# Where the sums of MLP weights are made: by transfers ahead of time, or on load, in a hybrid block on one core

## The chip, the core and the metric

The kernel runs on one core of a Trainium2 chip. The metric is the device time in microseconds (us) of one execution. It took 1217.34 us before the change, the median of three runs (1215.89 to 1218.22).

The engines go by the names of the profile: PE is TensorE (its weight loads are PEld), DVE VectorE, ACT ScalarE, POOL GpSimd, and SP the queue from which most transfers are issued. L633 is line 633 of the kernel.

## The reference

One block over a sequence of 1024 tokens with 1024 features, all in 32-bit floating point:

```python
h = rms_norm(x, norm1_g)
x = x + hybrid_mixer(h, ...)            # 8 heads of stick-breaking attention beside an RG-LRU
h = rms_norm(x, norm2_g)
x = x + sq_relu_mlp(h, w_up, w_down)

def hybrid_mixer(h, ...):
    proj = h @ w_in
    q, k, v, xl, gl = jnp.split(proj, ...)
    attn = stick_breaking_attention(rms_norm(q, ...), rms_norm(k, ...), v)
    lru = rg_lru(causal_depthwise_conv(xl, ...), ...) * jax.nn.gelu(gl)
    return jnp.concatenate([attn, lru], axis=-1) @ w_out

def sq_relu_mlp(h, w_up, w_down):
    return jnp.square(jax.nn.relu(h @ w_up)) @ w_down     # 1024 -> 4096 -> 1024
```

## The kernel before

Every product is made in three matmuls: each operand is split in a high part, rounded to TensorE's fast 32-bit type by ACT (L544), and a low part, the rest, by DVE or POOL (L60). A name ending in h or l (`sh_u`, `sl_u`) is such a part. A station (`s...`) is the operand that TensorE loads, a moving operand (`m...`) the one that streams.

The program has four stretches. To 155 us it normalizes x, projects and runs the LRU. From 155 to 462 us attention runs in head pairs, with the rest of the input projection and the gates of the LRU between its steps. From 462 to 566 us comes the output projection, and then the MLP to 1210 us.

The MLP is cut in two groups of 2048 hidden features, and each runs `up_group` and then `down_group`. The product of 2 x 2 blocks is made with seven block products in place of eight, so some products need sums of blocks of the weights. In w_up the blocks are called w(i, j, k): half i of the group's features, tile j of that half, half k of the inputs. `up_group` has four passes over j = 0 to 7:

- p1 (L657 on): stations `a` from w(0, j, 0) and w(0, j, 1), two quarter-products (12 matmuls each) per j.
- p6 and p7: stations `s`. `rs` takes w(1, j, 1) by a load and a ready sum of two blocks by another (L697); POOL adds the two (L698). p6 streams `t2`, p7 `t3`; the low part of half of `t3` is made on POOL.
- p4: stations `t`, a plain load for two j.
- p5 and b22: stations `u`. `ru` and `rv` take four loads, two of them ready sums (L735, L736), and POOL adds all in one instruction of 128x1024 (L737).

The eight sums U of a j are squared on ACT or POOL (L660, L662, L664). `down_group` runs seven products of 96 matmuls (pa, pb, pc); p6, p7 and p4 read ready sums of w_down, and POOL adds `rp` and `qp` (L767).

The ready sums lie in DRAM: `sum_u` and `sum_d`, 2 x 2 MB each for each group. `weight_sum(n)` makes them on POOL's own transfer queue, for each group 4 transfers of 2 MB for w_up and 4 for w_down: the first two copy a block of weights, the other two add a block to what was copied (`accum_op`). Eight of the sixteen, those for group 0, are the steps Y00 to Y07 of the attention part's table ORDER (L34). The other eight, for group 1, are issued in group 0: two in p6 (L699), two in p4 (L715), four in the down products p5 and p6 (L768). Each is issued behind the last POOL instruction that was marked.

`raw` tiles hold what is loaded: a pool of six buffers of 128x1024; split stations rotate through three pairs, moving operands through five. A scheduler orders each engine's instructions by a simulated timeline; in each queue they then run in that order.

The gates (G steps, `gate`, L478) multiply a projection by the row scales 1/rms. The scales lie in DRAM (`rs_d`); `rsb` holds them broadcast over the partitions, but only while the LRU runs, so each of the eight gate steps loads its half of them again into `gx` (L483) before DVE's multiply (L487).

Of the kernel before, what the change touches and what calls it, by code (L numbers as in the profile page):

```python
# [19 lines left out]
P = 128  # L20
S = 1024
# [12 lines left out]
ORDER = (  # L34
# [3 lines left out]
).split()  # L38
# [5 lines left out]
def kernel(ctx, tc, x, norm1_g, w_in, conv_w, conv_b, w_rg, b_rg, w_ig, b_ig,  # L44
# [85 lines left out]

    sums = {("u", g): dram.tile([2, 8, P, 512], F32, name=f"sum_u{g}") for g in range(2)}
    sums.update({("d", g): dram.tile([2, 8 * P, 512], F32, name=f"sum_d{g}") for g in range(2)})

    def weight_sum(n):
        m, g = (("u", 0), ("d", 0), ("u", 1), ("d", 1))[n // 4]
        i, k, dst = ((1, 0, 0), (0, 1, 1), (0, 0, 0), (1, 1, 1))[n % 4] if m == "u" else ((1, 1, 0), (0, 0, 1), (0, 1, 0), (1, 0, 1))[n % 4]

        def rows(w):  # L140
            return w.rearrange("j p c -> (j p) c") if len(w.shape) == 3 else w


        f = 16 * g + 8 * i
        src = rows(w_up[k, f:f + 8] if m == "u" else w_down[k, f * P:(f + 8) * P])
        with tc.issue_after(marked[0]):
            nc.gpsimd.dma_start(rows(sums[m, g][dst]), src, max_dma_last_dim=2048, **({"accum_op": ALU.add} if n % 4 > 1 else {}))

# [3 lines left out]
    hTl = hp.tile([P, KC, S], F32R, name="hTl")  # L152
    qkvE = pool(left1, "qkvE")
    wp = pool(left1, "wp", bufs=8)
    mp = pool(left1, "misc")
# [196 lines left out]
    lp = pool(lstack, "lru", bufs=2, side="right")  # L352
    rsb = lp.tile([P, S], F32, name="rsb", bufs=1)
    for ch in range(2):
# [124 lines left out]
    def gate(c, ch):  # L479
        s0 = 512 * ch  # L480
        y = mp.tile([P, 512], F32, tag="raw", name=f"gx{c}{ch}", bufs=2)
        hs = mp.tile([P, 512], F32, tag=("ks", "kl")[c % 2], name=f"hl{c}{ch}")
        nc.sync.dma_start(y, rs_row[:, s0:s0 + 512].broadcast_to([P, 512]))  # L483
        nc.sync.dma_start(hs, lru_d[c * P:(c + 1) * P, s0:s0 + 512])
        pd = proj_cols(gw[c // 2 * 2], c % 2, ch, f"pgl{c}{ch}")
        t = mp.tile([P, 512], F32, tag=("sq", "qs")[c % 2], name=f"ge{c}{ch}")
        nc.vector.tensor_tensor(y, pd, y, op=ALU.mult)  # L487
        nc.scalar.activation(t, y, AF.Square, scale=math.sqrt(0.044715))
        nc.vector.scalar_tensor_tensor(t, t, 1.0, y, op0=ALU.add, op1=ALU.mult)
        nc.scalar.activation(t, t, AF.Sigmoid, scale=c2)  # L490
        nc.gpsimd.tensor_tensor(hs, hs, y, op=ALU.mult)
        nc.gpsimd.tensor_tensor(hs, hs, t, op=ALU.mult)
        nc.sync.dma_start(mix_d[AW + c * P:AW + (c + 1) * P, s0:s0 + 512], hs)
# [13 lines left out]
    for op, *digits in ORDER:  # L507
# [5 lines left out]
        elif op == "A":  # L513
            attention(*arg, qkvs[arg[0]])
        elif op == "Y":
            weight_sum(10 * arg[0] + arg[1])
        elif op == "W":
            gate_w(*arg)
        else:
            gate(*arg)  # L520
# [123 lines left out]
    def up_group(g):  # L644
        SU = sums["u", g]

# [23 lines left out]
        for j in range(9):  # L670
# [7 lines left out]
            if held is not None:  # L678
                ps, st = held
                mm4(ps, st, 1, b21, False)  # L680
                relu2(j - 1, 0, ps)
            held = cur

# [10 lines left out]
        for j in range(8):  # L694
            r = raw(f"rs{g}{j}")
            nc.sync.dma_start(r[:, 0], w_up[1, 16 * g + 8 + j])
            nc.sync.dma_start(r[:, 1], SU[0, j])  # L697
            mark(nc.gpsimd.tensor_tensor(r[:, 0], r[:, 0], r[:, 1], **add))  # L698
            if g == 0 and j % 4 == 0:  # L699
                weight_sum(8 + j // 4)  # L700
            st = split(nc.vector, pair(stp, f"s{g}{j}"), r)
# [12 lines left out]
        for j in range(8):  # L714
            if g == 0 and j % 4 == 2:  # L715
                weight_sum(10 + j // 4)
            if j % 2 == 0:
# [11 lines left out]
        for j in range(9):  # L729
            cur = None  # L730
            if j < 8:
                r, q = raw(f"ru{g}{j}"), raw(f"rv{g}{j}")
                nc.sync.dma_start(r[:, 0], w_up[0, 16 * g + 8 + j])
                nc.sync.dma_start(q[:, 0], w_up[1, 16 * g + 8 + j])
                nc.sync.dma_start(r[:, 1], SU[1, j])  # L735
                nc.sync.dma_start(q[:, 1], SU[0, j])  # L736
                mark(nc.gpsimd.tensor_tensor(r, r, q, **add))  # L737
                st = split(nc.vector, pair(stp, f"u{g}{j}"), r)
# [14 lines left out]
    def down_group(g):  # L753
        SD = sums["d", g]

# [3 lines left out]
        def product(name, pss, src, unit, start):  # L759

            for k in range(0, 8, 2):
                r = raw(f"r{name}{g}{k}")
                nc.sync.dma_start(r, src[0](k))
                if len(src) > 1:
                    q = raw(f"q{name}{g}{k}")
                    nc.sync.dma_start(q, src[1](k))
                    mark(nc.gpsimd.tensor_tensor(r, r, q, **add))  # L767
                    if g == 0 and name != "p4" and k % 4 == 0:  # L768
                        weight_sum(12 + (2 if name == "p6" else 0) + k // 4)
                mv = split(nc.vector, pair(mvp, f"{name}{g}{k}"), r)  # L770
# [104 lines left out]
```

## Time and profile before

The profiled execution took 1218.14 us. Its span, from its first instruction to its last, is 1216.4 us; 1.7 us lie around it.

| | us |
|---|---|
| median of three runs | 1217.34 |
| profiled execution | 1218.14 |
| its span | 1216.4 |
| front to 155 us | 155.0, TensorE busy 138.25 |
| attention part | 307.0, TensorE busy 292.84 |
| output projection | 104.3, TensorE busy 95.78 |
| MLP group 0 | 332.87, TensorE busy 315.85 |
| MLP group 1 | 311.23, TensorE busy 305.84 |
| POOL busy | 586.5 of the span |
| granted TensorE clock | 0.969 of full speed |

Busy time adds up an engine's instructions; a row with a bracket, such as [8.83 <-issue], gives the idle time in front of an instruction and what ended it, "issue" where the profile shows nothing that the engine waited for. "DMA to landing" is the time from a transfer's issue to its last byte. The transfers of `weight_sum` land a median of 12.7 us (w_up) and 13.3 us (w_down) after their issue.

### The profile page before, as it was taken

What the parts mean: (1) busy time and instruction counts of PE and PEld (TensorE: products, weight loads), DVE (VectorE), ACT (ScalarE), POOL (GpSimd) and SP (SyncE); (2) the same over time, 40 slices, a digit from 0 to 9 for tenths busy, and PEclk for the clock granted to TensorE, in tenths of its full rate; (3) what the DMA queues carried; (4) which work ended last, traced back from release to release, by engine and by line L of the source; (5) the groups of instructions that cost most, each with busy time, mean ns of one, the idle gap of its engine ahead of it and who ended that gap; (6) DMA issues with size and microseconds to landing.
All of it is one profiled execution on the core that took longest, in us unless ns stands there. A gap on an engine that the chain in (4) does not pass through costs nothing.

```text
span 1216.4 us, 15273 instructions
## 1 busy us (share of the span) xinstructions
PE 1150.6 (95%) x5410; PEld 948.0 (78%) x5410; DVE 897.3 (74%) x1182; ACT 568.5 (47%) x991; POOL 586.5 (48%) x472
## 2 busy tenths in 40 slices
PE   7998899999999988998999989889999999999998
PEld 7976777789987766886888767678887887878887
DVE  6889997999898788226387769685843876699663
ACT  7554475665665564144433554233334335733331
POOL 1356764574355566102645746533317368483240
PEclk9999999799999978998999989989999999999999
DMA  8110026824505275200453788944412345442531
GB/s 262 48 49 35 18 96 130 227 66 145 122 5 112 89 256 181 101 1 35 141 188 130 201 241 287 224 142 139 141 35 87 122 144 191 158 148 73 193 132 69
DMA packets 91659, 157.05 MB, mean 129 GB/s; under 512 B 8848, under 2 KB 27328, under 8 KB 91584
## 3 DMA queue, kind: packets, MB, share of 16 engines
q1 hardware_dynamic: 79040, 122.54, 30.5%
q0 software_dynamic: 12544, 33.56, 11.8%
q8 instruction: 42, 0.69, 0.2%
q14 instruction: 33, 0.27, 0.1%
HBM read 145.58 MB, written 44.04 MB: 156 GB/s over the span
## 4 chain that ended last, share of the span: by engine, by line
PE 69%; DVE 13%; issue 8%; DMA 3%; POOL 3%; ACT 3%; SPq 0%; DVEq 0%; ACTq 0%; POOLq 0%
PE p L633 22%; PE pa L633 11%; PE pb L633 5%; PE pc L633 4%; PE pd L71 3%; PE pd L72 3%; PE pd L73 3%; PE po L71 3%; PE po L72 2%; PE po L73 2%; PE av L461 2%; PE z L432 2%; PE pw L452 2%; DVE g L441 2%; DVE sl_u L60 2%
## 5 line engine op out<-in xcount | busy, mean ns | idle before, releaser
L442 POOL TENSOR_TENSOR w<-w,g 128x128 f32<-128x128 f32 (+3 forms) x96 | 99.7, 1044 | 107.7 <-DVE g L441 52.7
L60 DVE TENSOR_TENSOR ml_p<-rp,mh_p 128x1024 fp32r<-128x1024 f32 x56 | 110.3, 1971 | 28.1 <-ACT mh_p L544 28.1
L441 DVE TENSOR_TENSOR_SCAN g<-g 128x128 f32<-128x128 f32 (+3 forms) x96 | 112.6, 1185 | 8.0 <-ACT g L436 5.4
L544 ACT CAST sh_p<-U 128x1024 fp32r<-128x1024 f32 x48 | 50.5, 1051 | 131.0 <-PE pa L633 59.2
L633 PE MATMUL pa<-mh_p,sl_p 128*128 128x512 f32 x256 | 100.7, 393 | 7.1 <-DVE sl_p L60 6.8
L767 POOL TENSOR_TENSOR rp<-rp,qp 128x1024 f32<-128x1024 f32 x24 | 69.0, 2876 | 70.3 <-DMA qp<-in_w_down_dram 39.8
L633 PE MATMUL pa<-ml_p,sh_p 128*128 128x512 f32 x256 | 100.3, 392 | 0.0
L633 PE MATMUL pa<-mh_p,sh_p 128*128 128x512 f32 x256 | 100.1, 391 | 0.0
L71 PE MATMUL pd<-wh_p,hTl 128*128 128x384 f32 x256 | 90.9, 356 | 7.3 <-DVE vv L206 5.0
L72 PE MATMUL pd<-wl_p,hTh 128*128 128x384 f32 x256 | 89.8, 351 | 0.1
L73 PE MATMUL pd<-wh_p,hTh 128*128 128x384 f32 x256 | 88.3, 345 | 0.0
L60 DVE TENSOR_TENSOR sl_p<-U,sh_p 128x1024 fp32r<-128x1024 f32 x38 | 63.4, 1668 | 30.7 <-ACT sh_p L544 30.7
L737 POOL TENSOR_TENSOR ru<-ru,rv 128x1024 f32<-128x1024 f32 x16 | 43.8, 2769 | 58.9 <-DMA rv<-sum_u 58.8
L544 ACT CAST mh_p<-rp 128x1024 fp32r<-128x1024 f32 x56 | 58.7, 1048 | 21.3 <-POOL rp L767 14.6
L633 PEld LDWEIGHTS pa<-mh_p,sl_p 128*128 128x128 f32 x256 | 48.5, 189 | 18.2 <-DVE sl_p L60 7.5
L662 POOL TENSOR_TENSOR U<-U 128x512 f32<-128x512 f32 x32 | 47.0, 1501 | 32.0 <-ACT U L660 32.0
L456 ACT CAST wth<-pw 128x512 fp32r<-128x512 f32 (+1 forms) x80 | 42.4, 545 | 38.0 <-PE pw L452 24.8
L436 ACT ACTIVATE g<-z 128x384 f32<-128x384 f32 (+3 forms) x96 | 47.8, 497 | 22.9 <-PE z L434 10.4
L71 PEld LDWEIGHTS pd<-wh_p,hTl 128*128 128x128 f32 x256 | 49.4, 193 | 11.0 <-DVE vv L206 6.7
L660 ACT ACTIVATE U<-U 128x512 f32<-128x512 f32 x48 | 30.0, 628 | 58.6 <-DVE U L721 31.1
L60 DVE TENSOR_TENSOR wtl<-pw,wth 128x512 fp32r<-128x512 f32 (+1 forms) x80 | 49.5, 629 | 9.5 <-ACT wth L456 8.9
L633 PEld LDWEIGHTS pa<-mh_p,sh_p 128*128 128x128 f32 x256 | 48.5, 189 | 10.2
(325 smaller groups left out, 3566.7 us busy)
## 6 DMA issues: line engine op xcount, KB each, us to landing
sum_u<-in_w_up_dram POOLq DMA_DIRECT2D x8, 2048.0 KB, 12.7
sum_d<-in_w_down_dram POOLq DMA_DIRECT2D x8, 2048.0 KB, 13.3
rp<-in_w_down_dram SPq DMA_DIRECT2D x32, 512.0 KB, 4.1
rp<-sum_d SPq DMA_DIRECT2D x24, 512.0 KB, 5.4
ra<-in_w_up_dram SPq DMA_DIRECT2D x16, 512.0 KB, 4.4
qp<-in_w_down_dram SPq DMA_DIRECT2D x16, 512.0 KB, 4.2
wr_p<-in_w_in_dram SPq DMA_DIRECT2D x24, 192.0 KB, 5.8
xt<-in_x_dram SPq DMA_DIRECT2D x8, 512.0 KB, 7.5
```

Source lines behind the costliest of these rows:

```text
L60: ins = eng.tensor_tensor(lo, src, hi.bitcast(F32), op=ALU.subtract)
L71: nc.tensor.matmul(ps, al, bh, start=start, stop=False)
L72: nc.tensor.matmul(ps, ah, bl, start=False, stop=False)
L73: nc.tensor.matmul(ps, ah, bh, start=False, stop=stop)
L436: nc.scalar.activation(g[:, :kn], z, AF.Sigmoid, scale=-1.0)
L441: nc.vector.tensor_tensor_scan(gr, gr, gr, g[:, kn:kn + 1], op0=ALU.mult, op1=ALU.bypass)
L442: mark(nc.gpsimd.tensor_tensor(w[:, :kn], w[:, :kn], g[:, 1:kn + 1], op=ALU.mult))
L544: nc.scalar.copy(hl[0], src)
L633: nc.tensor.matmul(ps, x_, y_, start=start and n == 0, stop=stop and n == 2, skip_group_check=True)
L662: mark(nc.gpsimd.tensor_tensor(c, c, c, op=ALU.mult))
L737: mark(nc.gpsimd.tensor_tensor(r, r, q, **add))
L767: mark(nc.gpsimd.tensor_tensor(r, r, q, **add))
```

## The change

The sums of w_up are no longer kept in DRAM. p6 loads the two blocks that made up the ready sum beside the third (a second raw tile `rq` per j, three loads of 256 KB for two), and POOL makes two adds of 128x512 (new L695, L696) for one. p5 loads four plain blocks; POOL adds them pairwise in 128x1024 (new L733) and then one half to the other (new L734). The sums of w_down stay transfers, for both groups now within the same group's up passes: two copies in p1 at j = 1 and 5, two accumulates in p6 at j = 1 and 5. None is left in the attention part nor in the down products. `rsb` moves to a pool that lives until the gates are done, the gates read it, and the eight loads of `gx` are gone.

```diff
-    "A000 A001 A002 Y00 A003 O1 A010 A013 A011 Y01 A012 I10 A100 A110 I11 Y02 A101 I12 A112 A111 I13 Y03 A103 W0 "
+    "A000 A001 A002 A003 O1 A010 A013 A011 A012 I10 A100 A110 I11 A101 I12 A112 A111 I13 A103 W0 A113 A102 G00 G10 "
...
+    def weight_sum(g, n):
+        i, k = ((1, 1), (0, 0), (0, 1), (1, 0))[n]
...
+        f = (16 * g + 8 * i) * P
         with tc.issue_after(marked[0]):
+            nc.gpsimd.dma_start(flat(sums[g][n % 2]), flat(w_down[k, f:f + 8 * P]), max_dma_last_dim=2048,
+                                **({"accum_op": ALU.add} if n > 1 else {}))
...
+    rsb = hp.tile([P, S], F32, name="rsb")
...
-    rsb = lp.tile([P, S], F32, name="rsb", bufs=1)
...
-        nc.sync.dma_start(y, rs_row[:, s0:s0 + 512].broadcast_to([P, 512]))
...
-        nc.vector.tensor_tensor(y, pd, y, op=ALU.mult)
+        nc.vector.tensor_tensor(y, pd, rsb[:, s0:s0 + 512], op=ALU.mult)
...
                 relu2(j - 1, 0, ps)
+                if j in (1, 5):
+                    weight_sum(g, j // 4)
...
-            r = raw(f"rs{g}{j}")
-            nc.sync.dma_start(r[:, 0], w_up[1, 16 * g + 8 + j])
-            nc.sync.dma_start(r[:, 1], SU[0, j])
+            r, q = raw(f"rs{g}{j}"), raw(f"rq{g}{j}")
+            nc.sync.dma_start(r[:, 1], w(1, j, 0))
+            nc.sync.dma_start(q[:, 1], w(0, j, 0))
+            nc.sync.dma_start(r[:, 0], w(1, j, 1))
+            nc.gpsimd.tensor_tensor(r[:, 1], r[:, 1], q[:, 1], **add)
             mark(nc.gpsimd.tensor_tensor(r[:, 0], r[:, 0], r[:, 1], **add))
-            if g == 0 and j % 4 == 0:
-                weight_sum(8 + j // 4)
+            if j in (1, 5):
+                weight_sum(g, 2 + j // 4)
...
-            if g == 0 and j % 4 == 2:
-                weight_sum(10 + j // 4)
...
-                nc.sync.dma_start(r[:, 0], w_up[0, 16 * g + 8 + j])
-                nc.sync.dma_start(q[:, 0], w_up[1, 16 * g + 8 + j])
-                nc.sync.dma_start(r[:, 1], SU[1, j])
-                nc.sync.dma_start(q[:, 1], SU[0, j])
-                mark(nc.gpsimd.tensor_tensor(r, r, q, **add))
+                nc.sync.dma_start(r[:, 0], w(1, j, 0))
+                nc.sync.dma_start(q[:, 0], w(1, j, 1))
+                nc.sync.dma_start(r[:, 1], w(0, j, 1))
+                nc.sync.dma_start(q[:, 1], w(0, j, 0))
+                nc.gpsimd.tensor_tensor(r, r, q, **add)
+                mark(nc.gpsimd.tensor_tensor(r[:, 1], r[:, 1], r[:, 0], **add))
...
-                    if g == 0 and name != "p4" and k % 4 == 0:
-                        weight_sum(12 + (2 if name == "p6" else 0) + k // 4)
```

The scheduler orders each engine's queue anew. POOL's rows around the start of group 1's p6, first of the kernel before (`rs` the sums, `ml_t...<-t3r` the low part of t3, U a square of p1):

```order
L662 TENSOR_TENSOR U<-U 128x512
L698 TENSOR_TENSOR rs_8636<-rs_8636 128x512
L698 TENSOR_TENSOR rs_8672<-rs_8672 128x512
L662 TENSOR_TENSOR U<-U 128x512 x2
L60 TENSOR_TENSOR sl_a_8569<-ra_8566,sh_a_8568 128x1024
L698 TENSOR_TENSOR rs_8708<-rs_8708 128x512
L662 TENSOR_TENSOR U<-U 128x512
L698 TENSOR_TENSOR rs_8744<-rs_8744 128x512
L698 TENSOR_TENSOR rs_8780<-rs_8780 128x512
L60 TENSOR_TENSOR ml_t_8627<-t3r_8624,mh_t_8626 128x1024
```

The same place after the change (`sum_d` is a transfer of `weight_sum`, the first row of it a copy, the second an accumulate):

```order
L695 TENSOR_TENSOR rs_8648<-rs_8648,rq_8649 128x512
L696 TENSOR_TENSOR rs_8648<-rs_8648 128x512
L656 TENSOR_TENSOR U<-U 128x512 x2
L60 TENSOR_TENSOR sl_a_8581<-ra_8578,sh_a_8580 128x1024
L695 TENSOR_TENSOR rs_8687<-rs_8687,rq_8688 128x512
L656 TENSOR_TENSOR U<-U 128x512
L142 DMA sum_d_94<-in_w_down_dram 1024x512
L696 TENSOR_TENSOR rs_8687<-rs_8687 128x512
L142 DMA sum_d_94<-in_w_down_dram 1024x512
L695 TENSOR_TENSOR rs_8727<-rs_8727,rq_8728 128x512
L60 TENSOR_TENSOR ml_t_8639<-t3r_8636,mh_t_8638 128x1024
```

Five sums stood ahead of t3's low part; now two whole sums, one half-made one and two transfers do, and the accumulate follows the copy with one add between them.

POOL's rows at the end of group 1's p5, before (`ru` the sums of p5, L800 the first subtraction of the down products, `rp` their first sum of weights):

```order
L737 TENSOR_TENSOR ru_9301<-ru_9301,rv_9302 128x1024
L662 TENSOR_TENSOR U<-U 128x512
L737 TENSOR_TENSOR ru_9343<-ru_9343,rv_9344 128x1024
L737 TENSOR_TENSOR ru_9385<-ru_9385,rv_9386 128x1024
L800 TENSOR_TENSOR U<-U 128x2x512
L767 TENSOR_TENSOR rp_9590<-rp_9590,qp_9592 128x1024
```

And after the change:

```order
L733 TENSOR_TENSOR ru_9344<-ru_9344,rv_9345 128x1024
L734 TENSOR_TENSOR ru_9301<-ru_9301 128x512
L656 TENSOR_TENSOR U<-U 128x512
L733 TENSOR_TENSOR ru_9387<-ru_9387,rv_9388 128x1024
L734 TENSOR_TENSOR ru_9344<-ru_9344 128x512
L734 TENSOR_TENSOR ru_9387<-ru_9387 128x512
L733 TENSOR_TENSOR ru_9430<-ru_9430,rv_9431 128x1024
L795 TENSOR_TENSOR U<-U 128x2x512
L734 TENSOR_TENSOR ru_9430<-ru_9430 128x512
L764 TENSOR_TENSOR rp_9636<-rp_9636,qp_9638 128x1024
```

A sum is now two instructions that don't stand side by side, and the last sum's second half comes behind the first subtraction of the down products (L795, before L800).

SP's rows around the gates in the attention part, before (`gx` the row scales, `hl` the LRU's result, `mix_d` stores):

```order
L484 DMA hl_3057<-lru_d 128x512
L163 DMA wr_p_2_3954<-in_w_in_dram 128x3x128
L469 DMA mix_d<-ob_1852 64x256
L483 DMA gx_3093<-rs_d 128x512
L163 DMA wr_p_3_3960<-in_w_in_dram 128x3x128
L493 DMA mix_d<-hl_3019 128x512
L469 DMA mix_d<-ob_1905 64x256
L469 DMA mix_d<-ob_1992 64x256
L483 DMA gx_3130<-rs_d 128x512
```

After the change:

```order
L479 DMA hl_3049<-lru_d 128x512
L465 DMA mix_d<-ob_1849 64x256
L488 DMA mix_d<-hl_3013 128x512
L465 DMA mix_d<-ob_1902 64x256
L479 DMA hl_3085<-lru_d 128x512
L488 DMA mix_d<-hl_3049 128x512
L479 DMA hl_3121<-lru_d 128x512
L488 DMA mix_d<-hl_3085 128x512
```

The loads of `gx` are gone, and the gates' loads and stores stand closer together.

More of the change, by code (lines that the diff above doesn't have):

```diff
@@ L129, with flat @@
     rs2 = const.tile([P, NT], F32, name="rs2")
[L133 to L145, printed above, removed]
+    sums = [dram.tile([2, 8 * P, 512], F32, name=f"sum_d{g}") for g in range(2)]
+    def weight_sum(g, n):
+        i, k = ((1, 1), (0, 0), (0, 1), (1, 0))[n]
+        def flat(w):
+            return w.rearrange("f c -> (f c)").rearrange("(a b) -> a b", b=512)
+        f = (16 * g + 8 * i) * P
         with tc.issue_after(marked[0]):
-            nc.gpsimd.dma_start(rows(sums[m, g][dst]), src, max_dma_last_dim=2048, **({"accum_op": ALU.add} if n % 4 > 1 else {}))
+            nc.gpsimd.dma_start(flat(sums[g][n % 2]), flat(w_down[k, f:f + 8 * P]), max_dma_last_dim=2048,
+                                **({"accum_op": ALU.add} if n > 1 else {}))
     left1 = ExitStack()
@@ L514 @@
             attention(*arg, qkvs[arg[0]])
-        elif op == "Y":
-            weight_sum(10 * arg[0] + arg[1])
         elif op == "W":
@@ L644, in up_group, with w @@
     def up_group(g):
-        SU = sums["u", g]
+        def w(i, j, k):
+            return w_up[k, 16 * g + 8 * i + j]
         def moving(name, srcs):
@@ L753, in down_group @@
     def down_group(g):
-        SD = sums["d", g]
+        SD = sums[g]
         def banks4(q, name):
```

4 rows, old and new, of the table ORDER are left out of this document.

## The prediction, made before the changed kernel ran

> **What bounds the kernel now.** The page's head and its row of busy times come first, then busy time by stage; in a row of stages the columns are the stretch, its length, the busy time (and instructions) of PE, PEld, DVE, ACT and POOL, the granted clock, the DMA share and GB/s.
>
> ```profile
> span 1216.4 us, 15273 instructions
> PE 1150.6 (95%) x5410; PEld 948.0 (78%) x5410; DVE 897.3 (74%) x1182; ACT 568.5 (47%) x991; POOL 586.5 (48%) x472
> 155.00:462.00 307.00, 292.84 (x1603) 240.29 (x1602) 267.51 (x481) 186.22 (x450) 168.25 (x229) 0.94 0.45 122
> 566.30:899.17 332.87, 315.85 (x1353) 258.76 (x1354) 231.07 (x182) 131.48 (x157) 163.32 (x76) 0.97 0.58 172
> 899.17:1210.40 311.23, 305.84 (x1337) 251.30 (x1336) 210.55 (x161) 125.20 (x148) 150.65 (x64) 0.99 0.38 127
> 855.65 21.76 PE pc L633 x96
> ```
>
> TensorE bounds it: 95% busy. The three stages are the attention part and the MLP's two groups of 1344 matmuls. The last row, from the chain of waits, is one MLP product that ran without a wait: 96 matmuls in 21.76 us, so a group needs 14 × 21.76 = 304.6 us. Group 1 takes 6.6 us more, group 0 28.2. The groups differ in that group 0 also carries the eight transfers that make group 1's weight sums. So the time a change can win is in group 0, and in whatever holds TensorE in the attention part.
>
> Group 0's loss by what TensorE waited for, and how often (the waits view: total us, times, longest), of 679.3 to 793.8, then the same for GpSimd, and the four accumulating transfers on GpSimd's timeline:
>
> ```profile
> PE p L633 <- DVE sl_u L60: 8.0, 2, 5.6
> PE pa L633 <- DVE sl_p L60: 6.8, 1, 6.8
> PE p L633 <- DVE U L741: 1.1, 1, 1.1
> PE pb L633 <- DVE sl_p L60: 0.9, 1, 0.9
> POOL sum_d L147 <- issue: 12.2, 1, 12.2
> POOL sum_u L147 <- issue: 8.8, 1, 8.8
> ...
> 675.68 1.35 POOL L147 DMA_DIRECT2D sum_u<-in_w_up_dram  x1
> 696.56 1.30 POOL L147 DMA_DIRECT2D sum_u<-in_w_up_dram  x1 [8.83 <-issue]
> 761.68 1.32 POOL L147 DMA_DIRECT2D sum_d<-in_w_down_dram  x1
> 780.98 1.31 POOL L147 DMA_DIRECT2D sum_d<-in_w_down_dram  x1 [12.19 <-issue]
> ```
>
> ```profile
> L147 POOL DMA_DIRECT2D sum_u<-in_w_up_dram x1: 1346/1346/1346, 675.7 to 675.7; - x1
> DMA to landing us min/median/max: 20.6/20.6/20.6
> ...
> 679.30:736.50 57.20, 48.16 (x196) 38.53 (x194) 42.18 (x27) 26.04 (x38) 31.30 (x17) 0.91 0.88 241
> 790.70:797.50 6.80, 3.72 (x9) 2.95 (x10) 6.80 (x6) 3.51 (x4) 4.51 (x2) 0.50 0.55 101
> ```
>
> TensorE's waits add up to 8.0 + 6.8 + 1.1 + 0.9 = 16.8 us. The transfer of 675.68 landed 20.6 us later, at 696.3, and GpSimd, which had reached the next accumulate, stood 8.83 us and went on at 696.56: **an accumulate issued while another is in flight holds GpSimd until that one lands**, and with it the weight sums (L737, L767) queued behind. TensorE then waits for the splits (sl_u, sl_p) of just those sums. After a wait the clock falls: 0.91 over 57.2 us costs 5.1 us, 0.50 over 3.72 busy us another 1.9. Group 0 loses 16.8 + 7.0 = 23.8 us by the transfers; the direct comparison, 332.87 − 311.23 = 21.6, agrees.
>
> **The change part by part.** The profiled run took 1218.1 us (span 1216.4 and 1.7 around it), 0.8 above the median of 1217.3; the sum is made against 1218.1.
>
> *1. The front: eight transfers and eight loads of row scales gone.*
>
> ```profile
>   DMA gx<-rs_d: 4.5, 3
>   PE pgl L71: 2.0, 1
> ...
> 200.20:203.60 3.40, 2.84 (x7) 2.26 (x8) 3.40 (x8) 2.58 (x6) 0.86 (x1) 0.50 1.08 199
> 230.90:248.00 17.10, 17.10 (x60) 12.37 (x60) 14.11 (x20) 10.34 (x24) 9.17 (x16) 0.50 0.86 198
> L147 POOL DMA_DIRECT2D sum_u<-in_w_up_dram x1: 1302/1302/1302, 225.4 to 225.4; - x1
> L147 POOL DMA_DIRECT2D sum_u<-in_w_up_dram x4 | 4.4, 1108 | 0.0
> L147 POOL DMA_DIRECT2D sum_d<-in_w_down_dram x4 | 4.2, 1056 | 0.0
> ```
>
> The first two rows belong to the gate's multiply (L487): DVE stood 4.5 us for gx, and TensorE 2.0 us behind it. With the scales in SBUF both go, and so does the half clock just behind it: 2.84 × ½ = 1.4. That is −3.4, and next in line is the gate's own matmul, which DVE has to wait for anyway. At 230.9 to 248.0 the clock is 0.50 for 17.1 us, 8.6 us lost, while the accumulate issued at 225.4 is in flight; but attention stages show such dips elsewhere too (0.94 over 307 us is 18 us), so I count 2.6 of these 8.6, between none and all. GpSimd saves 4.4 + 4.2 = 8.6 us of issuing, at 168 of 307 us busy: nothing. The order of gate work among the attention steps moves as well, which can cost what one more wait of this stage costs (5 us). **−6, between −12 and +5.**
>
> *2. Group 0's transfers for group 1 gone.* At most −23.8 (clock included). But group 1, which had none, shows what the same places cost with quiet queues:
>
> ```profile
> PE pb L633 <- DVE sl_p L60: 2.5, 2, 2.0
> PE p L633 <- DVE sl_u L60: 1.7, 2, 1.1
> ...
> 1056.40:1124.00 67.60, 65.12 (x279) 53.09 (x278) 64.17 (x40) 26.27 (x27) 38.85 (x14) 0.97 0.36 119
> ```
>
> These are 4.2 us of waits, and 0.03 × 67.6 = 2.0 of clock. Group 0 falls to about that: **−18, between −23.8 and −14** (the last if only the two held accumulates, 5.6 + 6.8, and a little clock go).
>
> *3. Four transfers per group in the first two passes (p1, p6).* Two copies issue in p1, where a step loads 512 KB by one raw tile, and two accumulates in p6 at j = 1 and 5: four steps of two quarter-products, 4 × 2 × 2.72 = 21.8 us apart (21.76 / 8 = 2.72), against the 20.6 us above. So the second accumulate holds GpSimd little or not at all. What they do to the loads beside them (DMA to landing of the sums' loads, L736, beside an accumulate and in group 1 without):
>
> ```profile
> DMA to landing us min/median/max: 8.0/9.1/10.2
> DMA to landing us min/median/max: 2.9/2.9/3.6
> ```
>
> In p6 each j now takes three loads of 256 KB and two raw tiles, so six tiles hold three j. In the steady state a tile comes free when its split is done, and with three stationary pairs behind, that is some five steps of 5.44 us before the same buffer's next sum must be split: 9.1 us and two adds fit. At the start they don't fit so well: the first sums of p6 that come after the t3 tiles get their buffers late, and the low part of t3 stands on GpSimd behind one of them. I take 2.5 us per group, the size of the longest such wait of group 1 (2.0) and half of the longest of group 0 (5.6). **+5 for both, between 0 and +28** (the upper end is the first rival).
>
> *4. Thirty-two more adds on GpSimd.*
>
> ```profile
> L737 POOL TENSOR_TENSOR ru<-ru,rv 128x1024 f32<-128x1024 f32 x8 | 21.0, 2629 | 30.5 <-DMA rv<-sum_u 30.5
> L698 POOL TENSOR_TENSOR rs<-rs 128x512 f32<-128x512 f32 x8 | 12.3, 1538 | 6.1 <-DMA rs<-sum_u 4.9 <-DVE ml_t L60 1.2
> L698 POOL TENSOR_TENSOR rs<-rs x16: 1284/1296/2301, 591.9 to 953.2; 128x512 f32<-128x512 f32 x16
> 1025.60 3.23 POOL L737 TENSOR_TENSOR ru<-ru,rv 128x1024 f32<-128x1024 f32 x1 [3.40 <-DMA rv<-sum_u]
> 1028.79 3.38 POOL L800 TENSOR_TENSOR U<-U 128x1024 f32<-128x1024 f32 x1
> L60 DVE TENSOR_TENSOR sl_u<-ru,sh_u x8: 1215/1340/3421, 1000.8 to 1043.2; 128x1024 fp32r<-128x1024 f32 x8
> ```
>
> A 128x512 add takes 1.30 us (median), so 16 more per group are 20.8 us on an engine that is busy 150.65 of group 1's 311.23. Of L737's 30.5 us of idle time 3.4 stand before the row of 1025.60; the other 27.1 lie before its first add, in p6, and cover eight adds there (10.4). In p5 it is busy almost without a break to 1028.8, when the last of eight sums is made; its split is due to begin by 1043.2, 14.4 us later. Eight adds and the L800 add, which now comes before the last one, take 10.4 + 3.4 = 13.8. The lead is used up and no more: **+1 per group, +2, between 0 and +18** (the second rival).
>
> The sums rounded otherwise, the scales' new place in memory and DMA bytes move no wait: part 1's load is replaced by nothing, and the new loads are priced under 3.
>
> Sum: −6 − 18 + 5 + 2 = −17, so 1218.1 − 17 = 1201.1 for a run like the profiled one, **1200** beside the median.
>
> **The rivals.**
>
> *The accumulates starve p6 (slower).* Part 2's stretch 679.30 to 736.50 had two accumulates beside loads: it lost 57.20 − 48.16 = 9.0 us of idle TensorE and 5.1 of clock, 14.1 us. If p6 fares as p5 did, each group pays 14.1. Then −3.4 in the front, −18 and +28.2: +7, **1224**. It decides once a load's 8 to 10 us plus two adds exceed what the buffers lead by. For it: the start of p6, and three loads where there were two. Against it: p6 asks 768 KB a step and p5 asked 1024, and the held issue, half of that loss, is gone.
>
> *GpSimd becomes the bound.* If the new adds take the 2.3 us of L698's longest in place of 1.30, eight of them and L800 are 21.8 us against the 14.4 us lead: 7.4 late, with a clock dip of 1.7 some 9 per group, so **1216**. For it: the split sl_u has a median of 1340 ns and a longest of 3421, and beside a busy GpSimd both engines' adds stretch. Against: DVE was busy 30.79 us of p5's 46.80 (below), and could lag 2 us on each of eight splits before it is short.
>
> ```profile
> 1009.60:1056.40 46.80, 45.06 (x198) 36.67 (x197) 30.79 (x28) 30.30 (x43) 30.50 (x13) 1.00 0.50 164
> ```
>
> The Trainium skill speaks against the change here: its page SBUF — State Buffer, section Who interferes with whom, says that a VectorE instruction with two SBUF inputs contends with a GpSimd instruction that reads SBUF, over a port pair that they share. The spread of sl_u, 3421 − 1215 = 2.2 us, agrees with that. By this rule alone, with all 32 new adds holding a split that TensorE waits for, the sum would be 32 × 1.30 = 42 us worse.
>
> *A copy in flight holds the next accumulate too.* No row shows that case. In group 1 the third transfer comes directly after the second, 9 to 13 us of flight; held, t3's low part comes late: 6.5 us and half clock. One group: **1208**.
>
> *The front gives more:* all 8.6 of the dip and little lost at p6: **1190**. *The change moves nothing* (the waits of group 0 come from elsewhere): 1217; the rows that name the held issues speak against.
>
> **How the numbers follow.** Forecast, 1194 to 1207: 0.45. Front gives more: 0.17. Held behind a copy: 0.10. GpSimd the bound: 0.13. Nothing moves: 0.05. Starved: 0.10. A difference under 0.2%, 2.4 us, is about what a measurement of this kernel can't tell from none. Faster than 1214.9: 0.45 + 0.17 + 0.10 and 0.11 of GpSimd's 0.13, 0.83. Within: 0.05 + 0.02 = 0.07. Slower: 0.10. The range leaves out the starved case and the far end of the front case: 1187 (1218 − 12 − 24 + 5) to 1218, 8 in 10.
>
> **What would show it.** Group 0's length should fall from 332.9 to about 315 to 320 and group 1's rise from 311.2 by 2 to 6. Right for part 1: no wait of L487's successor for a load, clock above 0.94. Right for part 2: no row in which GpSimd stands for "issue" in the down passes. Part 3 is wrong if TensorE waits for sl_s or for t3's split by more than 5 us in a group; part 4 if it waits for sl_u, and GpSimd's sums in p5 end after 1043 in group 1's old count. The forecast falls if the accumulates' landings (20.6 us) exceed the 21.8 us between their issues, since GpSimd is then held again, in both groups.

## The result, and the profile after

The changed kernel is **slower** by 0.9%: 1227.6 us median (1224.83 to 1232.92, seven runs) against 1218.08 (seven runs of before beside them); the ratio is 1.0089, with a 95% interval of 1.0066 to 1.0111. The forecast was 1200. The profiled execution has a span of 1224.3 us, 7.9 more than before.

The page's head and busy times after, then busy time by stretch (columns as in the prediction; here the LRU from its first product to the first attention scores, attention from there to the first output product, and the two groups from their first matmul to the next stage's; the last runs to the last MLP matmul):

```profile
span 1224.3 us, 15278 instructions
PE 1151.2 (94%) x5410; PEld 947.8 (77%) x5410; DVE 906.3 (74%) x1182; ACT 568.0 (46%) x991; POOL 633.6 (52%) x496
```

```profile
51.21:141.93 90.72, 81.91 (x343) 63.23 (x343) 78.69 (x111) 48.52 (x83) 54.02 (x60) 0.94 0.14 41
141.93:464.49 322.56, 299.94 (x1666) 248.28 (x1665) 289.40 (x517) 193.36 (x461) 177.25 (x235) 0.95 0.19 61
564.70:895.61 330.91, 316.50 (x1352) 259.03 (x1353) 229.87 (x182) 131.75 (x157) 188.79 (x88) 0.97 0.50 154
895.61:1220.34 324.73, 311.64 (x1345) 254.50 (x1343) 220.95 (x163) 125.19 (x148) 175.85 (x84) 0.98 0.50 154
```

The same two front stretches before:

```profile
53.40:137.25 83.85, 78.24 (x344) 60.51 (x343) 79.09 (x111) 48.80 (x83) 53.31 (x60) 1.00 0.16 48
137.25:466.02 328.77, 305.89 (x1665) 251.90 (x1664) 287.66 (x517) 193.98 (x461) 181.56 (x243) 0.93 0.43 117
```

Attention became 6.2 us shorter, but the LRU 6.9 longer. Between the same marks group 0 took 332.7 before (566.29 to 899.01) and 330.9 now: of the 18 us that it was to lose it lost 1.8. Group 1 took 313.4 (899.01 to 1212.39) and now 324.7, 11.3 longer. GpSimd is 47 us busier. What TensorE waits for in group 0, then in group 1 (waits view: total us, times, longest):

```profile
PE p L626 <- DVE sl_u L60: 5.3, 2, 2.9
PE p L626 <- DVE sl_s L60: 4.0, 1, 4.0
PE p L626 <- DVE sl_a L60: 4.0, 1, 4.0
PE p L626 <- POOL sl_t L60: 2.0, 1, 2.0
PE pa L626 <- POOL sl_p L60: 1.9, 1, 1.9
PE pa L626 <- DVE sl_p L60: 0.9, 1, 0.9
PE p L626 <- DVE U L738: 0.3, 1, 0.3
...
PE p L626 <- DVE ml_t L60: 3.5, 1, 3.5
PE pb L626 <- DVE sl_p L60: 3.2, 2, 2.3
PE p L626 <- DVE sl_a L60: 2.3, 1, 2.3
PE p L626 <- POOL sl_t L60: 2.2, 1, 2.2
...
```

The waits behind held accumulates are gone (6.8 for sl_p fell to 0.9), and others stand in their place: the splits of p6 (sl_s, ml_t) and of p4 (sl_t, made on GpSimd). The sl_a of group 0 is the first of the MLP and stood there before.

**The LRU.** SP's timeline of after shows it, then TensorE's first LRU product:

```profile
35.10 0.34 SPq L351 DMA_DIRECT2D rsb<-rs_d  x1
41.09 0.36 SPq L256 DMA_DIRECT2D rs_d<-rstd  x1
52.55 0.33 SPq L351 DMA_DIRECT2D rsb<-rs_d  x1
52.97 1.81 SPq L160 DMA_DIRECT2D wr_xl<-in_w_in_dram  x4
...
59.98 0.79 PE L71 MATMUL pxl<-hTh,wl_xl 128*128 128x512 f32 x1 [5.37 <-DVE vv L203]
```

The second rsb load needs the second store of the scales (issued at 41.09). SP stood for it until 52.55, and the loads of the LRU's weights stood behind it. With rsb in its new pool the scheduler puts these two loads ahead of wr_xl; before, the first wr_xl load stood ahead of both, and the same matmul waited 0.84 us:

```profile
51.26 0.34 SPq L163 DMA_DIRECT2D wr_xl<-in_w_in_dram  x1
51.70 2.59 SPq L355 DMA_DIRECT2D rsb<-rs_d  x2
57.64 0.50 PE L71 MATMUL pxl<-hTh,wl_xl 128*128 128x512 f32 x1 [0.84 <-DVE vv L206]
```

**p6.** DVE's timeline of after at the start of group 1's p6, and GpSimd's at the same place:

```profile
936.25 10.72 DVE L60 TENSOR_TENSOR ml_t<-h,mh_t 128x1024 fp32r<-128x1024 f32 x1 [1.48 <-ACT mh_t L537]
946.89 1.21 DVE L60 TENSOR_TENSOR sl_s<-rs,sh_s 128x1024 fp32r<-128x1024 f32 x1
```

```profile
935.62 0.77 POOL L142 DMA_DIRECT2D sum_d<-in_w_down_dram  x1
936.40 1.30 POOL L696 TENSOR_TENSOR rs<-rs 128x512 f32<-128x512 f32 x1
937.64 1.36 POOL L142 DMA_DIRECT2D sum_d<-in_w_down_dram  x1
938.43 1.88 POOL L695 TENSOR_TENSOR rs<-rs,rq 128x512 f32<-128x512 f32 x1
939.68 2.98 POOL L60 TENSOR_TENSOR ml_t<-t3r,mh_t 128x1024 fp32r<-128x1024 f32 x1
942.04 1.86 POOL L696 TENSOR_TENSOR rs<-rs 128x512 f32<-128x512 f32 x1
943.29 2.59 POOL L656 TENSOR_TENSOR U<-U 128x512 f32<-128x512 f32 x2
```

A split that takes 1.21 us alone took 10.72. GpSimd ran without a pause from 935.62 to 945.88 (943.29 + 2.59), and the split ended 1.09 us later, at 946.97: it got its turn only when GpSimd stopped. In after there are four such DVE instructions over 4.4 us, all in p6: 5.09, 5.76, 10.72 and 6.26 us. TensorE's two large waits of p6, 4.0 us for sl_s and 3.5 for ml_t, stand right behind the splits of 5.09 and 10.72 us.

### The profile page after: what moved, and what is told of

The parts are those of the page before. It is cut to its first block, busy times and chain, and to the rows that moved or that the text cites. A ratio compares the mean times of both kernels' runs of the same rounds, so it can differ in the third digit from the quotient of the medians.

```text
span 1224.3 us, 15278 instructions
## 1 busy us (share of the span) xinstructions
PE 1151.2 (94%) x5410; PEld 947.8 (77%) x5410; DVE 906.3 (74%) x1182; ACT 568.0 (46%) x991; POOL 633.6 (52%) x496
## 4 chain that ended last, share of the span: by engine, by line
PE 64%; DVE 15%; issue 6%; POOL 5%; DMA 5%; ACT 4%; SPq 0%; ACTq 0%; DVEq 0%; POOLq 0%
PE p L626 17%; PE pa L626 12%; PE pb L626 5%; PE pc L626 4%; PE po L71 2%; PE po L72 2%; PE po L73 2%; PE av L457 2%; PE pd L71 2%; DVE sl_p L60 2%; PE pd L72 2%; PE pd L73 2%; PE pw L448 2%; PE z L428 2%; POOL ru L733 2%
## 5 line engine op out<-in xcount | busy, mean ns | idle before, releaser
L438 POOL TENSOR_TENSOR w<-w,g 128x128 f32<-128x128 f32 (+3 forms) x96 | 102.8, 1078 | 106.4 <-DVE g L437 51.3
L60 DVE TENSOR_TENSOR sl_p<-U,sh_p 128x1024 fp32r<-128x1024 f32 x38 | 73.0, 1922 | 31.3 <-ACT sh_p L537 31.3
L72 PE MATMUL pd<-wl_p,hTh 128*128 128x384 f32 x256 | 90.4, 353 | 0.0
L537 ACT CAST mh_p<-rp 128x1024 fp32r<-128x1024 f32 x56 | 58.6, 1046 | 2.1 <-DMA rp<-in_w_down_dram 1.5
L733 POOL TENSOR_TENSOR ru<-ru,rv 128x1024 f32<-128x1024 f32 x16 | 41.6, 2599 | 33.1 <-DVE sl_t L60 16.6
L656 POOL TENSOR_TENSOR U<-U 128x512 f32<-128x512 f32 x32 | 43.3, 1378 | 26.5 <-ACT U L654 26.5
L626 PE MATMUL p<-mh_b,sl_a 128*128 128x512 f32 x128 | 50.8, 402 | 6.3 <-DVE sl_a L60 6.3
L626 PEld LDWEIGHTS pa<-mh_p,sh_p 128*128 128x128 f32 x256 | 48.5, 189 | 10.2
```

The costliest lines, as they stand in the source:

```text
L60: ins = eng.tensor_tensor(lo, src, hi.bitcast(F32), op=ALU.subtract)
L72: nc.tensor.matmul(ps, ah, bl, start=False, stop=False)
L438: mark(nc.gpsimd.tensor_tensor(w[:, :kn], w[:, :kn], g[:, 1:kn + 1], op=ALU.mult))
L537: nc.scalar.copy(hl[0], src)
L626: nc.tensor.matmul(ps, x_, y_, start=start and n == 0, stop=stop and n == 2, skip_group_check=True)
L656: mark(nc.gpsimd.tensor_tensor(c, c, c, op=ALU.mult))
```

## The experiments

Each kernel is compared by stretches of its profiled execution, from first matmul to first matmul as above (us), and by its median and ratio to the runs of before beside it. A stretch is from one execution, and the same code doesn't always take the same time: group 0 of before and of a (the same instructions in the same order on DVE, ACT and POOL) differ by 3.6 us, group 1 of after and of b by 1.8, and the attention part of before and of e by 6.2. So a difference of that size that rests on one row alone proves nothing.

| kernel | LRU | attention | group 0 | group 1 | median | ratio, 95% interval |
|---|---|---|---|---|---|---|
| before | 83.9 | 328.8 | 332.7 | 313.4 | 1218.08 | |
| after | 90.7 | 322.6 | 330.9 | 324.7 | 1227.6 | 1.0089 (1.0066 to 1.0111) |
| a: scales only | 90.2 | 323.5 | 336.3 | 313.5 | 1220.65 | 1.002 (0.9994 to 1.0045) |
| b: rsb loads later | 85.1 | 325.7 | 330.6 | 326.5 | 1224.14 | 1.006 (1.0028 to 1.0092) |
| c: adds on DVE | 90.2 | 322.8 | 329.8 | 327.2 | 1229.44 | 1.0098 (1.0068 to 1.0128) |
| d: transfers in front | 90.2 | 323.7 | 324.6 | 317.4 | 1215.21 | 0.9973 (0.995 to 0.9997) |
| i: small transfers | 90.5 | 320.7 | 326.7 | 319.6 | 1214.57 | 0.999 (0.997 to 1.0011) |
| g: no added adds | 90.3 | 322.5 | 326.7 | 316.1 | 1214.36 | 0.9988 (0.9966 to 1.001) |
| e: before, more adds | 84.5 | 322.6 | 339.4 | 321.6 | 1232.16 | 1.0128 (1.0091 to 1.0164) |
| f: all in front | 84.9 | 338.2 | 320.1 | 314.1 | 1218.26 | 1.0004 (0.998 to 1.0029) |
| k: late transfers | 84.3 | 325.2 | 323.8 | 314.5 | 1206.11 | 0.9903 (0.9876 to 0.9931) |
| l: and ACT's order | 84.3 | 325.5 | 314.4 | 313.4 | 1198.32 | 0.9859 (0.9826 to 0.9891) |
| n: copies on SP | 90.4 | 322.2 | 329.7 | 320.7 | 1219.57 | 1.0022 (1.0001 to 1.0043) |
| m: adds, clean base | 84.7 | 323.3 | 319.8 | 316.5 | 1203.93 | 0.9897 (0.9865 to 0.993) |

### a and b: the row scales

Edit a, in the kernel before:

```diff
+    rsb = hp.tile([P, S], F32, name="rsb")
-    rsb = lp.tile([P, S], F32, name="rsb", bufs=1)
-        nc.sync.dma_start(y, rs_row[:, s0:s0 + 512].broadcast_to([P, 512]))
-        nc.vector.tensor_tensor(y, pd, y, op=ALU.mult)
+        nc.vector.tensor_tensor(y, pd, rsb[:, s0:s0 + 512], op=ALU.mult)
```

> The kernel before with one part of the change alone: the row scales stay on chip for the gates, the eight gx loads go; all sums of weights as before. Theory (a queue held): SP's second load of rsb now stands ahead of four wr_xl loads and waits for the store of the scales, so the LRU stretch (to the first attention scores) starts its first product 4 to 5 us later and loses 5 to 7 us, while the gates save 2.0 us of waiting and 1.4 of clock: 1220 to 1223, slower. Rival (the LRU's loss comes from the removed transfers or from chance): no later start, 1213 to 1216.

Edit b, in the changed kernel, with the loads moved behind those of bd:

```diff
+    for ch in range(2):
+        with tc.issue_after(bd_last.ins):
+            nc.sync.dma_start(rsb[:, 512 * ch:512 * ch + 512], rs_row[:, 512 * ch:512 * ch + 512].broadcast_to([P, 512]))
```

> The changed kernel with the two rsb loads issued behind the wr_xl and bd loads on SP; nothing else edited. Theory (a queue held): the wait of 5.37 us at the first pxl product falls to about 1, the LRU stretch gets back 5 to 7 us, and the total is 1220 to 1223. Rival: the wait stays and the total is 1226 to 1229.

With the scales alone the LRU takes 90.2 in place of 83.9, and attention 323.5 in place of 328.8, though its eight transfers are still there, so these cost little. That the gates gave the gain is not shown: e, whose attention part is that of before, with the loads of gx and with the same order on DVE, ACT and POOL, took 322.6. By the medians a is 0.2% above before, 2.4 us, with an LRU 6.3 us longer, which would leave some 4 us gained elsewhere. The median of a, 1220.65, is where it was expected, but its interval holds no change too. In b, SP's and TensorE's timelines read:

```profile
44.13 0.37 SPq L256 DMA_DIRECT2D rs_d<-rstd  x1
52.09 3.09 SPq L160 DMA_DIRECT2D wr_xl<-in_w_in_dram  x4
...
58.12 1.07 SPq L359 DMA_DIRECT2D rsb<-rs_d  x2
...
59.75 0.50 PE L71 MATMUL pxl<-hTh,wl_xl 128*128 128x512 f32 x1 [2.11 <-DVE vv L203]
```

The wait falls from 5.37 to 2.11 us, not to 1, and the LRU from 90.7 to 85.1, with DVE and ACT in the same order as in after. The queue's order is the cause. The total fell by 3.5 and lies between the two expectations. Attention took 3.2 us more than in after, which is within what the same code shows from one execution to another.

### c: the adds on DVE

```diff
-            nc.gpsimd.tensor_tensor(r[:, 1], r[:, 1], q[:, 1], **add)
+            nc.vector.tensor_tensor(r[:, 1], r[:, 1], q[:, 1], **add)
...
-                nc.gpsimd.tensor_tensor(r, r, q, **add)
-                mark(nc.gpsimd.tensor_tensor(r[:, 1], r[:, 1], r[:, 0], **add))
+                mark(nc.gpsimd.tensor_tensor(r, r, q, **add))
+                nc.vector.tensor_tensor(r[:, 1], r[:, 1], r[:, 0], **add)
```

> The changed kernel with the 32 additional 128x512 adds on DVE in place of GpSimd. Theory (GpSimd's back-to-back adds hold DVE's splits): the splits of 10.7, 6.3 and 5.1 us in p6 fall below 3.5, TensorE's waits in p6 and p5 shrink by half, both groups together lose 8 to 16 us: 1212 to 1220. Rival (the loads beside the accumulates are late): the waits in p6 stay, and DVE has 20 us more work per group: 1226 to 1236.

Half right: no split takes over 3.5 us any more, with the same transfers. The time did not fall. DVE's queue now holds adds that wait for their loads, with the splits behind them; by the line's view of c:

```profile
L695 DVE TENSOR_TENSOR rs<-rs,rq x16: 676/693/3037, 596.0 to 969.7; 128x512 f32<-128x512 f32 x16
  DMA rq<-in_w_up_dram: 33.8, 10
```

DVE stood 33.8 us for rq, and TensorE's longest wait in p5 rose to 6.0 us for sl_u. So c takes the holds away and brings waits of its own; it doesn't price the holds.

### d and i: where the transfers stand, and their bytes

Edit d gives the eight transfers the places Y00 to Y07 and takes them out of p1 and p6. Edit i leaves them where the change put them, at an eighth of the size, with the full copies in front and seven eighths of the accumulates left out:

```diff
-    def weight_sum(g, n):
+    def weight_sum(g, n, rows=8):
...
-                    weight_sum(g, j // 4)
+                    weight_sum(g, j // 4, 1)
...
-                weight_sum(g, 2 + j // 4)
+                weight_sum(g, 2 + j // 4, 1)
```

> The changed kernel with its eight w_down transfers at the places Y00 to Y07 of the attention part, none in the MLP; the adds on load stay. Theory (GpSimd's adds hold DVE): DVE splits over 5 us remain, the MLP gains less than 5 us, the attention part pays 2 to 6: 1224 to 1230. Rival (loads late beside the accumulates): GpSimd's waits for loads in p6 go, the MLP gains 10 us or more: 1215 to 1220.

> The changed kernel with the four transfers per group at the same places of the up passes, but of 256 KB each in place of 2 MB; the full copies for them stand in the attention part, and seven eighths of the accumulates are left out. GpSimd's order in p1 and p6 stays, the moved bytes nearly go. Theory A (a transfer's issue, followed by a run of GpSimd instructions without a pause, holds DVE's splits to the end of the run): DVE instructions of 5 to 11 us remain in p6, and both groups stay within 4 us of the changed kernel's 330.9 and 324.7. Theory B (bytes: loads late beside the transfers, or descriptors of many packets): no split over 4 us, GpSimd's waits for rq shrink, and the groups fall to the 324.6 and 317.4 that they took with the transfers in the attention part.

Taking the transfers out of the up passes gives 6.4 and 7.3 us, and attention pays 1.1; the total is where the rival had it, and no DVE instruction of the MLP takes over 3.5 us. Taking away seven eighths of their bytes alone gives 4.2 and 5.2, so two thirds of the price goes with the bytes. A is wrong as the main cause: an issue with a run of adds behind it is not enough. B's total came, with a rest: one split of 4.91 us stayed, behind a small copy. But i does not tell late loads from held splits. GpSimd's waits for rq fell (from 5.7 to 2.4 us before p5 in group 0, from 13.5 to 3.5 in group 1), and three of the four held DVE instructions went too; in group 1, where the same run of adds follows, none over 3.6 us was left.

### g and e: the adds

Edit g leaves the 32 added adds out, so each sum of w_up lacks a block. Edit e puts adds that nobody reads into the kernel before:

```diff
+            nc.gpsimd.tensor_tensor(U[:, j, 1], r[:, 1], r[:, 1], **add)
             mark(nc.gpsimd.tensor_tensor(r[:, 0], r[:, 0], r[:, 1], **add))
...
-                mark(nc.gpsimd.tensor_tensor(r, r, q, **add))
+                nc.gpsimd.tensor_tensor(r, r, q, **add)
+                mark(nc.gpsimd.tensor_tensor(q[:, 1], r[:, 1], r[:, 0], **add))
```

> The changed kernel without the 32 additional 128x512 adds: each sum of w_up lacks one block; loads, buffers and transfers as they are. Theory (GpSimd's time is what binds): GpSimd 21 us less busy per group, the held splits shorten, both groups gain 5 to 9 us each: 1212 to 1218. Rival (loads beside the accumulates bind): the waits for sl_s and t3 in p6 stay, 1223 to 1228.

> The kernel before with 32 more 128x512 adds on GpSimd that nobody reads, one behind each sum of p6 (into a free part of U) and of p5 (into rv); loads and transfers as before. Group 1 has no transfers, so it prices the adds alone. Theory (an add on GpSimd costs by what it holds): group 1 rises from 313.4 by 3 to 6, about what the run with the transfers in the attention part showed (317.4). Rival (adds alone are hidden, that rise came from the third load): group 1 within 1.5 of 313.4.

Without the adds the groups fall by 4.2 and 8.6, and the total is in the expected range; with 32 adds and nothing else they rise by 6.7 and 8.2, more than expected. **The adds are not hidden.** But e charges more than the adds. In its group 1, which has no transfer, TensorE's longest wait is one of 4.7 us at the end of p5, and this is what stands in front of it (waits view of e, 1028 to 1046):

```profile
DVE ml_p L60 <- ACT mh_p L544: 9.6, 1, 9.6
ACT mh_p L544 <- DMA rp<-in_w_down_dram: 9.4, 1, 9.4
PE p L633 <- DVE U L743: 4.7, 1, 4.7
```

ACT's cast of the first block of w_down (mh_p) waits for its load, which was issued late: SP's loads in front of it stood 13.7 us for rv (L735; two waits), the buffer that e's added add of p5 writes and so keeps. DVE stands for that cast, with the U behind it. So 4.7 of the 8.2 us come from a buffer and an order, and what is left, 3.5, is near the 4.0 of d.

### f, k and l: versions meant to be faster

Edit f is the kernel before with all sixteen transfers in the attention part and the scales as in b.

> A version meant to be better than both: the kernel before, with all sixteen transfers in the attention part (copies and accumulates in turn), the row scales on chip and their loads behind the wr_xl loads on SP. No transfer is issued in the MLP and no add is new. Theory: group 0 falls from 332.7 to 314 to 319, group 1 stays at 313, the attention part takes 323 to 330: 1195 to 1206. Rival (sixteen transfers slow the attention part as eight slowed group 0): attention over 335, total 1207 to 1218.

Group 0 without any transfer and without added adds takes 320.1, the measure of what the transfers in it had cost: 12.6 us. But attention pays 9.4, the rival's case, so f gains nothing.

Edit k leaves before's eight in front and spreads the rest; a small GpSimd add holds each back until its product runs:

```diff
+LATE = {(0, "p3"): 10, (0, "p7"): 11, (0, "p2"): 12, (0, "p4"): 14, (1, "p3"): 13, (1, "p7"): 15}
...
+                if k == 2 and (g, name) in LATE:
+                    mark(nc.gpsimd.tensor_tensor(tick, mv[1][:, 0, 0:1].bitcast(F32), mv[1][:, 1, 0:1].bitcast(F32), **add))
+                    weight_sum(LATE[g, name])
```

> A second version meant to be better than both: the kernel before, its first eight transfers in the attention part as they are, its other eight moved: two copies stay in group 0's p6, the rest goes one by one to down products with few sums on GpSimd (group 0's p3, p7, p2 and p4, group 1's p3 and p7), 21.8 us apart, each behind a small GpSimd add that waits for a split of that product. The row scales are kept on chip with their loads behind the wr_xl loads. No add on load. Theory (what costs is an accumulate issued while another is in flight, and a GpSimd run behind an issue): group 0 falls from 332.7 to 316 to 322, group 1 to 313 to 317, LRU 85, attention 323 to 326: 1197 to 1207. Rival (moved bytes cost wherever they go): group 0 over 326, total 1210 to 1220.

1206.1: faster than both, in the expected range; group 0 a little above it. f and k keep one large wait in group 0, at the end of p5 (waits view of k, 690 to 703):

```profile
ACT mh_p L545 <- DMA rp<-in_w_down_dram: 6.5, 1, 6.5
PEld p L635 <- DVE sl_u L61: 6.2, 1, 6.2
PE p L635 <- DVE sl_u L61: 5.8, 1, 5.8
DVE ml_p L61 <- ACT mh_p L545: 4.7, 1, 4.7
```

ACT and DVE stand for the first block of w_down, and the next sl_u stands behind that on DVE. Edit l issues that cast behind the last cast of p5:

```diff
-                mv = split(nc.vector, pair(mvp, f"{name}{g}{k}"), r)
+                mv = split(nc.vector, pair(mvp, f"{name}{g}{k}"), r, last_hi[0] if name == "p1" and k == 0 else None)
...
+            with tc.issue_after(behind):
+                hi = nc.scalar.copy(hl[0], src)
```

> The version with the late transfers and one edit more: ACT's cast of the down products' first block of w_down (mh_p) is issued behind the cast of the last sum of p5 (sh_u). In group 0 that cast stands ahead of a sh_u in the version with the late transfers and waits 6.5 us for its load, and TensorE waits 5.8 us for the split behind it, though no transfer is in flight. Theory (this order, not the held accumulates, makes the last 7 us of group 0's loss): the wait of 5.8 us goes with its half clock of 1.7, group 0 falls from 323.8 to 315 to 318: 1196 to 1201. Rival (the sum ru itself is late): the wait stays, 1204 to 1208.

The wait is gone, group 0 takes 314.4, and **the median is 1198.3 us, 1.4% below before**. An order in ACT's queue was worth 9.4 us of group 0 in these executions and 7.8 between the medians (5.4 by the two ratios to before). It had hidden behind the held accumulates: in before ACT waited 4.5 us for the same load, and no wait of TensorE followed from it.

### n and m: the hold, and the adds on the clean base

Edit n issues the two copies on SP; the accumulates stay:

```diff
-            nc.gpsimd.dma_start(flat(sums[g][n % 2]), flat(w_down[k, f:f + 8 * P]), max_dma_last_dim=2048,
+            (nc.gpsimd if n > 1 else nc.sync).dma_start(flat(sums[g][n % 2]), flat(w_down[k, f:f + 8 * P]), max_dma_last_dim=2048,
```

> The changed kernel with the two copies of each group issued on SP, behind the same station's load; the accumulates stay on GpSimd, adds and bytes stay. Theory (a transfer issued on GpSimd, with a run of GpSimd instructions behind it, holds DVE): the split of 5.09 us at the start of group 0's p6, which followed a copy, is gone, p6/p7 of group 0 falls from 53.4 to 49 to 51.5; the splits behind the accumulates (5.76, 10.72, 6.26) may stay. Rival (the adds or bytes hold it): it stays, and p6/p7 with it.

The split of 5.09 us that followed a copy is gone, as is the one of 10.72. But p6 of group 0 takes 54.1 us, where the theory had 49 to 51.5: a DVE subtraction of 4.79 us (634.09), in GpSimd's run behind an accumulate (631.40), stands ahead of a split sl_s, and TensorE waits 3.4 us for it. Group 1 gains 4.0, the total 8 against after.

Edit m puts the change's adds on load on the base of l: only the sums of w_up differ, adds and one more load per j in p6 in place of eight transfers.

> The changed kernel's adds on load on the clean base: its four transfers for group 0 in the attention part and those for group 1 one by one in group 0's last four down products, each behind a small GpSimd add, the rsb loads behind wr_xl on SP, the cast of w_down's first block behind the last sh_u on ACT. Beside the best version so far only the sums of w_up differ: adds on load in place of eight transfers. Theory (the adds cost by themselves): both groups 3 to 8 us longer than 314.4 and 313.4, the attention part 1 to 2 shorter: 1203 to 1213. Rival (adds are hidden once orders are right): 1195 to 1200.

The groups take 5.5 and 3.0 us longer than in l, attention 2.1 less: 1203.9 against 1198.3. This prices adds on load, less what the eight transfers cost, with all else in order: 8.5 us for both groups, a fifth of the 42 us that a hold of TensorE by every one of them would have cost.

## Why the prediction was wrong, step by step

The sum said −17 and the runs say +10. Of these 27 us 8.7 are in the term of the new transfers, 6.9 in the row scales, which had no term, 6.5 in the adds and 5.4 in group 0's old transfers. So no one step failed alone; the price of the transfers in p1 and p6 was the furthest off.

- **Group 0's old transfers: term −18, measured −12.6.** The waits were named, and the held accumulates vanished. But I let group 0 fall to what group 1 shows. f shows 320.1, 12.6 us less: ACT's mh_p in front of a sh_u, waiting for its load, was late next. With that order mended l takes 314.4, 18.3 less, so the size was right for a kernel with one more edit. One wait was also read wrongly. I put both large waits down to sums that came late behind a held accumulate. That holds for sl_p (6.8 us). The wait of 5.6 us for sl_u stood behind a split that was itself slow, as the splits of p6 are in after. Its sum was made by 685.8, and it began 1.6 us after the accumulate of 696.56 and ended 1.1 us after GpSimd's run behind it:

```profile
698.13 9.80 DVE L60 TENSOR_TENSOR sl_u<-ru,sh_u 128x1024 fp32r<-128x1024 f32 x1 [0.44 <-ACT sh_u L544]
```

- **The front: −6 for attention, measured −6.2** (328.8 to 322.6). That it came out so close is partly luck, since the same code took 328.8 in before and 322.6 in e. The step that failed is the one that wasn't taken: rsb's new pool lets its loads issue earlier, and SP's order puts them ahead of wr_xl. I wrote that the scales' new place moves no wait. It moved the queue: +6.9 in the LRU.
- **Transfers in p1 and p6: term +5, measured +13.7** (after less d, 6.4 and 7.3). The bounds held it, the value didn't. I priced one late buffer at the start of p6, 2.5 us a group, and no slow split. What the runs show there is splits of 5.09 and 10.72 us with waits of 4.0 and 3.5 us behind them, where d waits 1.6 us for sl_s in group 1 and not at all in group 0; a lower clock is in it too (group 1 had 0.98, in d 1.00). Two thirds of the price go with the bytes (i). The sign that I gave, more than 5 us of waits for sl_s or t3 in a group, did not show.
- **Adds: term +2, measured +8.5** (d against f and before: 4.5 and 4.0), and 8.5 by m against l. I had found GpSimd idle 27 us in p6 and a lead in p5 that was just used up. Neither held. The first sl_s of p6 is late in group 1 (1.6 us in d, 1.4 in m; no such wait in before or l), although GpSimd has a long idle piece later in p6. And p5, which I had priced at 1 us per group, is not covered either: in m's group 0 TensorE waits 4.3 us there, 2.9 for sl_u and 1.3 for U, and l has no such wait.
- **Rivals.** The starved p6 had the sign and nearly the total (1224) at a chance of 0.10; its mechanism, loads late beside the accumulates, is in the 9.4 of 13.7 us that i takes away, and how much of these is loads is open. GpSimd as the bound was a part too, at 8.5 us and not the 18 of that rival. The copy that holds the next accumulate did not happen: GpSimd went from copy (935.62) to accumulate (937.64) with one add between.

Sum by the runs: attention −6.2, LRU +6.9, group 0's old transfers −12.6, new transfers +13.7, adds +8.5: +10.2 before rounding; the first LRU product stood 2.2 us earlier in this execution, for no reason that the change gives: +8.0, against a span 7.9 longer. The terms are steps from kernel to kernel, so that they add up proves nothing. And the parts overlap: taken in the other order, the adds are worth 12.8 us (after less g) and the transfers 9.4 (g against f and before).

What stays open: how much of the transfers' price in p6 is hold and how much is late loads in each group, what the gates' loads cost in attention, and why the same attention code takes 6 us more in one execution than in another.

## What to carry to other kernels

Before counting a wait as won, look for what is late just behind it in the in-order queues of each engine: here a cast that waited for its load took the place of a removed stall, and one line of order was worth 9.4 us beside the stall's 12.6. A tile that moves to another pool changes when its loads may issue, and with it what stands behind them in the transfer queue. Idle time covers new work only if it lies where the work is due: read it per pass, and price an added instruction by adding it alone, in a place where it keeps no buffer longer (e's adds kept rv). Before a stretch's gain is put down to an edit, see how far apart two executions of the same code lie.

## What was not expected of the hardware

An accumulating transfer issued by GpSimd while another is in flight held the engine (8.83 and 12.19 us in before, 10.16 and 16.04 in a). In after, with 28 us between the accumulates of a group (606.85 and 635.34, 937.64 and 966.05), it held nothing.

A DVE instruction with two inputs in SBUF can be held to the end of a whole run of GpSimd instructions. In the traces of before, of after and of the twelve experiments every DVE instruction over 4.4 us, up to 10.72, lay in a run of GpSimd instructions without a pause that had a transfer's issue in it, and most ended 1.1 us behind the run's last instruction. Where no transfer was issued beside the sums (d's MLP), runs of the same adds held no DVE instruction over 3.5 us; there the two engines took turns. Not every run with an issue held one: a copy at 746.03 in before did not. An issue in the run was needed in these traces and didn't suffice, and what decides was not found. The Trainium skill, SBUF — State Buffer, section Who interferes with whom, has the one that issues second blocked until the first instruction is done; the rows agree for single instructions (in d a split that began with a GpSimd add of 2.42 us, at 710.3, took 3.48 us and ended 1.1 us behind it), and 10.72 us is more than any one GpSimd instruction there took.
